# A transformer layer with 32 experts: fetching the first expert's rows before the last block of rows is routed, and reading four sums of an expert together

## The chip, the cores and the metric

The kernel runs on one core of one Trainium2 chip. The metric is device microseconds of one execution, lower is better. Three runs of the kernel before took 2155.97, 2157.39 and 2163.31 us (median 2157.39). One more execution was profiled.

## The reference

One decoder layer on 1024 rows (tokens) of 1024 numbers, all in float32. The part that matters here is the second half: a router picks 4 of 32 experts for each row, and each expert is a gated feed-forward layer over the rows that chose it.

```python
h = rms_norm(x, norm1_g) * (1.0 + scale1) + shift1
proj = h @ w_in                                  # then two kinds of attention
x = x + gate1 * (concat([o_a, o_b]) @ w_out)
h2 = rms_norm(x, norm2_g) * (1.0 + scale2) + shift2
logits = h2 @ w_router + b_router
top_val, top_idx = lax.top_k(logits, 4)          # of 32 experts
gates = softmax(top_val)
# for each expert e, on the rows xe that chose it:
gu = xe @ w_gate_up[e] + b_gate_up[e]            # 1024 -> 2048
g, u = minimum(gu[:, :1024], 7), clip(gu[:, 1024:], -7, 7)
act = (u + 1) * (g * sigmoid(1.702 * g))
y_e = act @ w_down[e] + b_down[e]                # 1024 -> 1024
x = x + gate2 * sum over the chosen experts of gates * y_e
```

## The kernel before

The kernel has four stages: the input projection, attention, a loop over eight blocks of 128 rows, and a loop over the 32 experts. On PE, ACT, DVE and SP (which issues the large loads) instructions run in the order in which the code is written (`tc.manual_schedule`). POOL's order is not written out, a scheduler chooses it from the dependences. Within its engine every instruction runs in order, and whoever waits holds up all that stands behind it.

**The block loop** (L1008 to L1050, class `Block` from L853). Per block b, PE makes the output projection (`products`, L872: 48 matmuls of 512 columns), DVE adds the residual (`add`, L882), the second norm's root is taken by POOL (the power at L111, called from `add`), `logits` (L915) gives the router's scores and the four best, and `places` (L938) works out at which place of each expert's list the row stands. A one-hot matrix `hot` (L948) marks which place of expert 0's list each row takes. `listed` (L958) multiplies it with three columns `tg` (row number minus 1024, gate, one) and adds this up over all eight blocks in the PSUM tile `p0`. `counted` (L970) updates the counts, `scattered` (L980) writes (row, gate) pairs into the table `tab` in HBM by four indirect DMAs from POOL. `rows_out` (L911) stores the block's normalized rows `h2` in `h2d` in HBM. These steps of block b are spread over the two following iterations. The tile `pay` holds what the scatters read. It has three buffers, so its first writer in block b, a POOL `iota` (L944), waits until the scatters of block b-3 have ended.

**Between the loops** (L1051 to L1089, then L1343 to L1352). The last block is routed, expert 0's list is read from `p0` (three small DVE operations for each piece of the list, L965 to L968), the experts are sorted by their counts (`key` to `order`, L1071 to L1089: the first expert to run is always expert 0, with room for 172 rows), and expert 0's rows are gathered from `h2d` by two indirect DMAs from POOL, 128 and 44 rows (`stage_g`, L1139). `stage_t` (L1161) transposes them on PE, ACT and DVE split them into a high and a low half (`xx`, L1177 and L1178), POOL makes a bf16 copy `xb` (L1179).

**The expert loop** (L1355 to L1360, `expert`, L1206). Each expert's weights come as 12 chunks of 1 MB: ten into a ring of six buffers (`eraw`), two (`draw`) into buffers of their own. ACT turns half a chunk at a time into a rounded copy `hb` (L826), DVE takes the remainder `ha` (L813). Buffers are freed by that, and SP's next load waits for it (`pump`, L833, called from `done`). PE then runs five groups of `products` (L1186: 64 matmuls on `hb`, L1196, and 32 times two on `ha`, L1202), and between the fourth and the fifth the "plain half": four of the eight output pieces of the down projection straight from `draw` (L1252), 64 matmuls in two rounds `kh` over pieces j of 0 to 3. The four sums lie in one PSUM tile `pg`, two to a bank. In the second round ACT reads the pieces 0 and 1 into `yl` as soon as they are complete (L1263), and the pieces 2 and 3 after their own matmuls. The tile framework orders reads and writes by tile, so PE's matmuls for j of 2 wait for the reads of j of 0 and 1. PSUM is handed out as four tiles of two banks in turn (`banks`, L1116). `between` calls `stage_t` of the next expert, and `later` puts the last transposes and the scatter of an expert into the next one.

At the end a loop over rows that found no room (L1372) runs as many times as a register loaded at L1371 says, here not at all.

## Time and profile before

| | us |
|---|---|
| median of three runs | 2157.39 |
| profiled execution | 2155.82 |
| span of its instructions | 2154.0 |
| PE busy, of the span | 2046.7 (95%) |
| DVE, ACT, POOL busy | 1631.7, 1357.8, 481.7 |
| share of the 16 DMA engines, 862 to 2100 us | 0.96, at 318 GB/s |

The span runs from the first to the last instruction. The attention ends near 585 us, the block loop runs to 719 us, the first expert's first product starts at 745.96 us, the last scatter is issued at 2142 us. PE is the busiest engine. A busy PE says little about its speed, since matmuls overlap and the granted clock has two levels (1.2 and 2.4 GHz: 0.5 and 1.0 in the views). So the places where PE waits, and the stretches at the lower clock, are what to look for.

### The profile page before, as it was taken

Reading aid. Unit: us, or ns where it says so; the run is one execution under the profiler, and the core shown is the slowest. Engines: PE = TensorE matmul, PEld = TensorE weight load, DVE = VectorE, ACT = ScalarE, POOL = GpSimd, SP = SyncE. Lnnn points to the kernel's source line nnn. Section 1 sums busy time; section 2 is a strip of 40 time slices with the busy share of each in tenths; the row PEclk is TensorE's granted clock in tenths of the full one; section 3 lists DMA queues with packets and bytes.
Section 4 is the critical chain, followed back from the end, with each engine's and each line's share of the span. In section 5 each row is a group of like instructions: output and inputs, shape, how many; then the busy total and the mean of one; then the engine's idle time right before and its main releaser. Section 6 shows DMA issues by size and latency. Waiting matters only on the chain.

```text
span 2154.0 us, 43837 instructions
## 1 busy us (share of the span) xinstructions
PE 2046.7 (95%) x16922; PEld 1914.8 (89%) x16922; DVE 1631.7 (76%) x2838; ACT 1357.8 (63%) x2391; POOL 481.7 (22%) x466
## 2 busy tenths in 40 slices
PE   6999999999999699999999999999999999999997
PEld 6877778998887599999998999999999999999996
DVE  6587765776666778788787877878878878878884
ACT  3522314777643367677677677777877777768774
POOL 2245532111013411112111222112111211211211
PEclk9999999999999799999999999999999999999998
DMA  8267886442233498899799999989999999999993
GB/s 296 67 161 220 217 237 164 112 114 70 90 129 145 158 338 293 268 337 343 268 295 347 289 315 317 324 296 349 309 321 300 355 319 330 325 332 322 332 321 81
DMA packets 273655, 549.53 MB, mean 255 GB/s; under 512 B 31796, under 2 KB 31812, under 8 KB 273316
## 3 DMA queue, kind: packets, MB, share of 16 engines
q1 hardware_dynamic: 251507, 490.61, 67.4%
q0 software_dynamic: 21936, 56.09, 11.2%
q8 instruction: 134, 2.20, 0.4%
q14 instruction: 78, 0.63, 0.1%
HBM read 501.84 MB, written 44.78 MB: 254 GB/s over the span
## 4 chain that ended last, share of the span: by engine, by line
PE 61%; ACT 5%; DMA 3%; DVE 3%; issue 2%; POOL 1%; POOLq 0%; SPq 0%; ACTq 0%; DVEq 0%
PE gu L1196 30%; PE gu L1202 13%; PE gu L1252 10%; PE gu L1285 2%; ACT hb L826 2%; PE gu L1174 2%; PE po L605 1%; ACT yl L1263 1%; DMA eraw<-in_w_down_dram 1%; DMA eraw<-in_w_gate_up_dram 1%; PE pss L567 1%; DMA tab<-pay,sli 1%; PE pt L598 1%; POOL tab L982 1%; DVE ha L813 0%
## 5 line engine op out<-in xcount | busy, mean ns | idle before, releaser
L813 DVE TENSOR_TENSOR ha<-eraw,hb 128x1024 bf16<-128x1024 f32 x640 | 760.0, 1240 | 7.7 <-ACT hb L826 7.7
L826 ACT ACTIVATE hb<-eraw 128x1024 fp32r<-128x1024 f32 x640 | 634.1, 1050 | 21.2 <-DMA eraw<-in_w_down_dram 15.3
L1196 PE MATMUL gu<-xx,hb 128*128 128x256 f32 (+13 forms) x4096 | 586.3, 299 | 2.2 <-DVE xx L1178 2.2
L1196 PEld LDWEIGHTS gu<-xx,hb 128*128 128x128 f32 x4096 | 552.9, 189 | 2.6 <-DVE xx L1178 2.4
L1202 PEld LDWEIGHTS <-ha 128*128 128x128 bf16 x5120 | 310.6, 97 | 11.8 <-issue 1.5
L1252 PE MATMUL gu<-ay,draw 128*128 128x128 f32 (+19 forms) x2048 | 277.9, 292 | 36.4 <-ACT yl L1263 32.9
L1252 PEld LDWEIGHTS gu<-ay,draw 128*128 128x128 f32 x2048 | 260.5, 192 | 44.5 <-ACT yl L1263 39.7
L1202 PE MATMUL gu<-xb,ha 128*128 128x128 bf16 (+19 forms) x4096 | 271.6, 224 | 0.0
L1216 ACT ACTIVATE tb<-gu,bcol 128x128 f32<-128x128 f32 (+19 forms) x512 | 156.9, 369 | 89.8 <-PE gu L1202 80.8
L1182 POOL DMA_INDIRECT out_dram<-y,slot x47 | 79.7, 1695 | 404.9 <-ACT y L1286 263.0
L1146 POOL DMA_INDIRECT xg<-h2d,slot x47 | 65.9, 1401 | 393.0 <-PE gu L1174 86.8
L1196 PE MATMUL gu<-ax,hb 128*128 128x256 f32 (+13 forms) x1024 | 144.5, 298 | 0.0
L1276 ACT ACTIVATE tb<-gu,bcol,g2c 128x128 f32<-128x128 f32 (+19 forms) x128 | 56.3, 465 | 132.4 <-PE gu L1202 104.8
L1196 PEld LDWEIGHTS gu<-ax,hb 128*128 128x128 f32 x1024 | 137.4, 188 | 0.6
L571 DVE CUSTOM_DVE_ANT_0 p<-pss,bias 128x1024 f32<-128x1024 f32 (+7 forms) x128 | 94.4, 755 | 52.1 <-ACT p L580 23.5
L1277 DVE SCALAR_TENSOR_TENSOR ay<-gu,g2c,tb 128x128 f32<-128x128 f32 (+19 forms) x128 | 46.2, 362 | 113.9 <-ACT tb L1276 113.9
L1258 POOL CAST ab<-ax 128x512 bf16<-128x512 f32 (+19 forms) x64 | 69.7, 1094 | 263.7 <-ACT ax L1256 263.7
L605 PE MATMUL po<-vsb,pT 128*128 128x64 f32 (+1 forms) x864 | 111.3, 275 | 2.9 <-ACT pT L599 1.4
L605 PEld LDWEIGHTS po<-vsb,pT 128*128 128x128 f32 x864 | 105.4, 194 | 5.8 <-ACT pT L599 2.0
L580 ACT ACTIVATE p<-p,mn 128x1024 f32<-128x1024 f32 (+7 forms) x128 | 98.6, 773 | 11.9 <-DVE mn L571 11.2
L111 POOL TENSOR_TENSOR rrs<-vrs,nhalf 128x8 f32<-128x8 f32 (+2 forms) x48 | 66.1, 1377 | 169.6 <-DVE vrs L109 167.8
L459 PE MATMUL pp<-wh,hb 128*128 128x512 f32 x240 | 100.5, 419 | 0.0
(275 smaller groups left out, 3080.6 us busy)
## 6 DMA issues: line engine op xcount, KB each, us to landing
eraw<-in_w_gate_up_dram SPq DMA_DIRECT2D x256, 1024.0 KB
draw<-in_w_down_dram SPq DMA_DIRECT2D x64, 1024.0 KB
eraw<-in_w_down_dram SPq DMA_DIRECT2D x64, 1024.0 KB
wraw<-in_w_ada_dram SPq DMA_DIRECT2D x32, 512.0 KB
wraw<-in_w_in_dram SPq DMA_DIRECT2D x23, 512.0 KB
hb<-in_w_ada_dram SPq DMA_DIRECT2D x16, 512.0 KB
qd<-tt POOLq DMA_DIRECT2D x32, 256.0 KB, 3.7
kd<-tt POOLq DMA_DIRECT2D x32, 256.0 KB, 4.0
```

The source lines that it names most:

```text
L459: nc.tensor.matmul(pp, hh[b][:, k], wh[:, kk], start=(k == 0), stop=False)
L571: nc.vector.tensor_tensor_reduce(p[:, :n], pss[:, :n], bias[:, (NB - 1 - ib) * P:(NB - 1 - ib) * P + n], -1.0, 3.0e38, OP.add, OP.min, mn)
L580: nc.scalar.activation(p, p, AF.Exp, bias=self.mn[c], scale=-1.0, accum_out=self.l[:, c:c + 1])
L605: nc.tensor.matmul(self.po[:, :w], self.pT[:, k], vsb[self.br][:, k, self.h * w:(self.h + 1) * w], start=(k == 0), stop=(k == self.ib))
L813: nc.vector.tensor_tensor(parts[t][1], raws[c][:, 2 * q:2 * q + 2], parts[t][0].bitcast(F32), OP.subtract)
L826: nc.scalar.activation(h_, raws[c][:, 2 * q:2 * q + 2], AF.Copy)
L1182: nc.gpsimd.indirect_dma_start(out=out, out_offset=bass.IndirectOffsetOnAxis(ap=sl.bitcast(I32)[:n, 0:1], axis=0), in_=y[:n], in_offset=No ...
L1196: nc.tensor.matmul(pg[j // 2][:, j % 2, :max(256, 2 * C)], w[k][0][:, j * P:(j + 1) * P], xk[k], start=(k == 0), stop=False)
L1202: nc.tensor.matmul(pg[j // 2][:, j % 2, C:2 * C], w[k][1][:, j * P:(j + 1) * P], xb[:, k], start=False, stop=(k == KT - 1))
L1216: nc.scalar.activation(t[:, j], p[:, j, C:2 * C], AF.Identity, bias=bc[:, f + j:f + j + 1], scale=1.0)
L1252: nc.tensor.matmul(place(j), raw[:, k, j * P:(j + 1) * P], a[:, 4 * kh + k], start=(kh + k + j % 2 == 0), stop=(kh == 1 and k == 3 and j % ...
L1258: nc.gpsimd.tensor_copy(ab[:, f], ah[:, f, :C].bitcast(F32))
```

## The change

Three edits.

1. **Expert 0's rows come in two parts.** `listed` now adds up the blocks 0 to 6 only, before the last block is routed. Inside the last `add` the sums are copied to `sums0`, and two lists `early0`, `early1` are made from them (`slots_of`). Two indirect DMAs gather the rows of these lists at once into `xg0`. Places that belong to a row of block 7, or to none, fetch rows 1024 and up of `h2d`, which are zeros. `stage_0` then adds up in PSUM the transposes of the gathered rows (matmuls with the identity) and block 7's own rows times its one-hot matrix (`cur.h2` times `cur.hot`), 32 matmuls in place of 16 transposes. The complete list (`slots0`), the sorting of the experts and the rest follow after that. For it, the last block's `h2` and `hot` and the gathered rows live in `hb` buffers, and `pay` and `sli` have eight buffers, one per block. The rows of `h2d` that belong to block 7 are set to zero once, early.
2. **The plain half's four sums are read together**, after the loop over j.
3. **The register of the overflow loop is loaded before expert 5**, not at the end.

```diff
@@ table, add, places, listed, counted @@
+                nc.sync.dma_start(h2d[S - P:S, :], z)
...
+            def slots_of(sums, tiles):
+
+                for i, (t0, n) in enumerate(BLOCKS0):
+                    sl, c = tiles[i], 3 * i
+                    nc.vector.tensor_scalar(sl[:n, 0:1], sums[:n, c:c + 1], pcol[:n], float(S), op0=OP.add, op1=OP.add)
+                    nc.vector.scalar_tensor_tensor(sl.bitcast(I32)[:n, 0:1], sums[:n, c + 2:c + 3], pneg[:n], sl[:n, 0:1],
+                                                   op0=OP.mult, op1=OP.add)
...
                     nc.scalar.activation(sq, self.x1[:, c], AF.Square, accum_out=self.s2[:, n:n + 1])
+                    if mid:
+                        mid()
...
-                    self.h2 = ro.tile([P, D], F32, name="h2", bufs=1)
+                    self.h2 = ro.tile([P, D], F32, name="h2", bufs=1) if self.b < NB - 1 else slot(False).bitcast(F32)
...
-                    pay = (sm if self.b < NB - 1 else rt).tile([P, TOPK, 2], F32, name="pay")
+                    pay = rt.tile([P, TOPK, 2], F32, name="pay", bufs=NB)
...
-                                         stop=(self.b == NB - 1 and i == len(BLOCKS0) - 1))
-                    if self.b == NB - 1:
...
+                                         stop=(self.b == NB - 2 and i == len(BLOCKS0) - 1))
...
-                    self.sli = (sm if self.b < NB - 1 else rt).tile([P, TOPK], I32, name="sli")
+                    self.sli = rt.tile([P, TOPK], I32, name="sli", bufs=NB)
@@ after the block loop @@
             cur.products(1, range(PZ, 8))
+            pv.listed()
             cur.turn_x1(0)
-            cur.add(1)
-            pv.listed()
+            early = [rt.tile([P, 2], F32, name=f"early{i}") for i in range(len(BLOCKS0))]
+
+            def fetch_list():
+                nc.vector.tensor_copy(sums0, p0[:, :3 * len(BLOCKS0)])
+                slots_of(sums0, early)
+
+            cur.add(1, fetch_list)
+            xg0 = []
+            for (t0, n), sl in zip(BLOCKS0, early):
+                xg0.append(slot(False).bitcast(F32))
+                nc.gpsimd.indirect_dma_start(out=xg0[-1][:n], out_offset=None, in_=h2d,
+                                             in_offset=bass.IndirectOffsetOnAxis(ap=sl.bitcast(I32)[:n, 0:1], axis=0))
...
             cur.places()
-            cur.listed()
             pump(2)
             cur.counted()
             pump(4)
-
-
-            pc = ps3.tile([P, 512], F32, name="po")[:, :E]
...
+        def stage_0(st):
+
+            st["x"] = operand(C0, "xx", "xb")
+            bc = st["bc"]
+            nc.vector.tensor_mul(bc[:, 2 * KT:], bc[:, 2 * KT:], g2c)
+            pts = [banks().rearrange("p g (k c) -> p (g k) c", k=4) for _ in BLOCKS0]
+            for (t0, n), xg, pt in zip(BLOCKS0, xg0, pts):
+                for k in range(KT):
+                    nc.tensor.matmul(pt[:, k, :n], xg[:n, k * P:(k + 1) * P], ident[:n, :n], start=(k % 4 == 0), stop=False)
+            for (t0, n), pt in zip(BLOCKS0, pts):
+                for k in range(KT):
+                    nc.tensor.matmul(pt[:, k, :n], cur.h2[:, k * P:(k + 1) * P], cur.hot[:, t0:t0 + n],
+                                     start=False, stop=(k % 4 == 3))
+                operand_of(st, t0, n, pt)
@@ expert @@
-                    if kh and j % 2:
-                        if j == 1:
-                            yl = ap_.tile([P, 4, C], F32, name="yl")
-                        for f in (j - 1, j):
-                            nc.scalar.activation(yl[:, f], place(f), AF.Identity,
-                                                 bias=bc[:, 2 * KT + f:2 * KT + f + 1], scale=g2c[:, f:f + 1])
-                    if j == 1:
                         done()
+                if kh:
+                    yl = ap_.tile([P, 4, C], F32, name="yl")
+                    for f in range(4):
+                        nc.scalar.activation(yl[:, f], place(f), AF.Identity,
+                                             bias=bc[:, 2 * KT + f:2 * KT + f + 1], scale=g2c[:, f:f + 1])
@@ between the loops @@
-        st = stage_g(0)
+        st = {"C": C0, "bc": cols.pop(0), "blocks": BLOCKS0, "slots": slots.pop(0)}
+        stage_0(st)
         cur.scattered()
-        stage_t(st, 0)
-        stage_t(st, 1)
+        pl = banks()[:, 0]
+        for i, (t0, n) in enumerate(BLOCKS0):
+            nc.tensor.matmul(pl[:, 3 * i:3 * i + 3], cur.hot[:, t0:t0 + P], cur.tg, start=(i == 0), stop=(i == len(BLOCKS0) - 1))
+        nc.vector.tensor_add(sums0, sums0, pl[:, :3 * len(BLOCKS0)])
+        slots_of(sums0, slots0)
...
+        pc = banks()[:, 0, :E]
...
+            if i == 5:
+                n_over = nc.values_load(tot[0:1, 0:1], min_val=0, max_val=P)
```

How this moves instructions is shown at three places. First ACT, in the plain half of the first expert, in the kernel before (`yl`: the four sums, `hb`: half chunks of weights, `xx`: the next expert's operand).

```order
L1256 ACTIVATE ax<-ay 128x4x172
L1263 ACTIVATE yl<-gu,bcol,g2c 128x172 x2
L826 ACTIVATE hb<-eraw 128x1024
L1263 ACTIVATE yl<-gu,bcol,g2c 128x172 x2
L826 ACTIVATE hb<-eraw 128x1024
```

And in the changed kernel, whose line numbers are its own:

```order
L1269 ACTIVATE ax<-ay 128x4x172
L836 ACTIVATE hb<-eraw 128x1024
L1276 ACTIVATE yl<-gu,bcol,g2c 128x172 x4
L836 ACTIVATE hb<-eraw 128x1024
L1175 ACTIVATE xx<-gu 128x8x128
```

All four reads now stand behind one half chunk and in front of the next.

Second POOL, from the last blocks of the block loop to the first expert, before (`rr`: the norm's power, `tab`: the scatters of a block, `xg`: the gathers of expert 0's rows).

```order
L982 DMA tab<-pay,sli 36864x2 x4
L111 TENSOR_TENSOR rr_7253<-vr_7251,nhalf 128x1
L982 DMA tab<-pay,sli 36864x2 x4
L111 TENSOR_TENSOR rr_7418<-vr_7416,nhalf 128x1
L982 DMA tab<-pay,sli 36864x2 x4
L1146 DMA xg<-h2d,slots_2975 128x1024
L1146 DMA xg<-h2d,slots_2976 44x1024
L982 DMA tab<-pay,sli 36864x2 x4
```

The same place in the changed kernel (the gathers write `hb` buffers):

```order
L988 DMA tab<-pay,sli 36864x2 x4
L111 TENSOR_TENSOR rr_7255<-vr_7253,nhalf 128x1
L988 DMA tab<-pay,sli 36864x2 x4
L1072 DMA hb<-h2d,early_7413 128x1024
L111 TENSOR_TENSOR rr_7429<-vr_7427,nhalf 128x1
L1072 DMA hb<-h2d,early_7414 44x1024
L988 DMA tab<-pay,sli 36864x2 x8
```

The gathers stand ahead of the last eight scatters, around the last block's power. The `iota` of `pay`, which stood between a block's scatters and the next power four times, is at the program's start for all blocks.

Third SP at the end of the block loop, with the semaphores that each load or store waits for, before.

```order
L892 DMA out_dram<-osb 128x1024 [waits DMAHW2_49,DVE_49]
L913 DMA h2d<-h_7441 128x1024 [waits DMAHW7_49,DVE_49]
L1107 DMA bcol<-in_b_exp_t_dram 128x24 [waits DMAHW0_49]
L796 DMA eraw_7562<-in_w_gate_up_dram 128x4x512 [waits DMAHW4_49,DMAHW1_49,DMAHW6_49,PE_49,Activation_49]
L796 DMA eraw<-in_w_gate_up_dram 128x4x512 [waits DVE_49]
```

And in the changed kernel:

```order
L904 DMA out_dram<-osb 128x1024 [waits DMAHW3_49,DVE_49]
L925 DMA h2d<-hb 128x1024 [waits DMASW7_49,DMAHW0_49,DMASW6_49,DVE_49]
L1102 DMA bcol<-in_b_exp_t_dram 128x24 [waits DMAHW1_49]
L806 DMA eraw_7546<-in_w_gate_up_dram 128x4x512 [waits DMAHW5_49,DMAHW2_49,DMAHW7_49,PE_49,Activation_49]
L806 DMA eraw<-in_w_gate_up_dram 128x4x512 [waits DVE_49]
```

The order is the same, but the store of block 7's rows has two more waits (DMASW7 and DMASW6, DMAs issued by POOL): both gathers must have ended, since they read the same HBM tensor.

## Rows read from the trace of the kernel before

**Rows 1.** The page's costliest groups: busy us, mean ns, idle before, releaser

```profile
L1252 PE MATMUL gu<-ay,draw 128*128 128x128 f32 (+19 forms) x2048 | 277.9, 292 | 36.4 <-ACT yl L1263 32.9
```

**Rows 2.** Who waited for whom, PE, 760 to 2100: total, times, longest

```profile
PE gu L1252 <- ACT yl L1263: 32.1, 31, 3.2
PE gu L1252 <- DVE ay L1238: 2.5, 2, 2.1
```

**Rows 3.** Timeline of PE, plain half of the fourth expert: start, us, instruction, idle before

```profile
929.13 2.05 PE L1252 MATMUL gu<-ay,draw 128*128 128x128 f32 x16 [0.90 <-ACT yl L1263]
931.01 0.94 PE L1174 MATMUL gu<-ident,xg 128*128 128x128 f32 x8
931.88 4.06 PE L1196 MATMUL gu<-ax,hb 128*128 128x256 f32 x32
```

**Rows 4.** Timeline of ACT and DVE at the same place

```profile
931.22 0.81 ACT L1263 ACTIVATE yl<-gu,bcol,g2c 128x128 f32<-128x128 f32 x2 [1.20 <-PE gu L1252]
932.86 1.13 ACT L1177 ACTIVATE xx<-gu 128x1024 fp32r<-128x1024 f32 x2
...
934.28 1.34 DVE L1178 TENSOR_TENSOR xx<-gu,xx 128x1024 fp32r<-128x1024 f32 x2
```

**Rows 5.** Busy time by stretch: PE, PEld, DVE, ACT, POOL, clock, DMA, GB/s

```profile
921.70:962.30 40.60, 39.70 (x411) 38.86 (x409) 35.48 (x49) 31.97 (x54) 6.01 (x6) 1.00 1.01 355
...
756.00:776.00 20.00, 20.00 (x167) 19.63 (x166) 16.52 (x21) 15.15 (x22) 0.00 (x0) 1.00 1.05 383
```

**Rows 6.** Who waited for whom, ACT, 760 to 2100

```profile
ACT hb L826 <- DMA eraw<-in_w_down_dram: 15.3, 10, 7.6
```

**Rows 7.** Who waited for whom, POOL, 560 to 720

```profile
POOL pay L944 <- DMA tab<-pay,sli: 10.5, 4, 3.2
```

**Rows 8.** Timeline of DVE in one block of the loop

```profile
654.78 0.17 DVE L109 TENSOR_SCALAR vrs<-ss 128x4 f32<-128x4 f32 x1 [1.25 <-ACT sq L694]
657.06 0.16 DVE L115 TENSOR_TENSOR qr<-rr 128x1 f32<-128x1 f32 x1 [2.10 <-POOL rr L111]
```

**Rows 9.** Timeline of PE in the same block

```profile
658.67 0.58 PE L960 MATMUL p<-tg,hot 128*128 128x3 f32 x4 [2.31 <-DVE tg L955]
```

**Rows 10.** Who waited for whom, PE, 540 to 760

```profile
PE p L960 <- DVE tg L955: 6.2, 5, 2.3
```

**Rows 11.** Busy time by stretch, two iterations of the block loop

```profile
656.00:674.00 18.00, 15.69 (x82) 13.08 (x81) 11.06 (x35) 6.17 (x22) 6.23 (x9) 0.91 0.40 147
...
692.00:710.00 18.00, 16.59 (x77) 14.03 (x76) 12.29 (x43) 4.89 (x14) 6.26 (x10) 0.81 0.42 138
```

**Rows 12.** Timeline of DVE and POOL between the two loops

```profile
720.46 0.69 DVE L886 TENSOR_TENSOR osb<-osb,t 128x512 f32<-128x512 f32 x1
730.41 0.22 DVE L966 SCALAR_TENSOR_TENSOR slots<-p,pneg,slots 128x1 int32<-128x1 f32 x1
...
722.44 0.57 POOL L111 TENSOR_TENSOR rr<-vr,nhalf 128x1 f32<-128x1 f32 x1 [2.17 <-DVE vr L109]
732.27 1.02 POOL L1146 DMA_INDIRECT xg<-h2d,slots  x1 [2.11 <-DMA h2d<-h]
733.60 1.66 POOL L1146 DMA_INDIRECT xg<-h2d,slots  x1 [0.31 <-DVE mcum L978]
```

**Rows 13.** Timeline of PE between the two loops

```profile
738.03 1.08 PE L1174 MATMUL gu<-ident,xg 128*128 128x128 f32 x4 [4.04 <-DMA xg<-h2d,slots]
741.49 2.25 PE L1174 MATMUL gu<-ident,xg 44*128 44x44 f32 x12 [2.37 <-DMA xg<-h2d,slots]
745.96 6.86 PE L1196 MATMUL gu<-xx,hb 128*128 128x344 f32 x32 [2.22 <-DVE xx L1178]
```

**Rows 14.** Chain of waits between the two loops: start, us, what

```profile
743.20 1.03 ACT xx L1177
```

**Rows 15.** Timeline of SP's issues at the end of the block loop

```profile
728.09 0.32 SPq L913 DMA_DIRECT2D h2d<-h  x1
729.27 5.57 SPq L796 DMA_DIRECT2D eraw<-in_w_gate_up_dram  x2
```

More of the change, by code (lines that the diff above doesn't have):

```diff
@@ L658, in hybrid_layer @@
             slots0 = [rt.tile([P, 2], F32, name=f"slots0{i}") for i in range(len(BLOCKS0))]
+            sums0 = rt.tile([P, 3 * len(BLOCKS0)], F32, name="sums0")
             dgc = rt.tile([P, 1], F32, name="dgc")
@@ L942, in places @@
                     nc.vector.reciprocal(self.den, self.den)
-                    pay = (sm if self.b < NB - 1 else rt).tile([P, TOPK, 2], F32, name="pay")
+                    pay = rt.tile([P, TOPK, 2], F32, name="pay", bufs=NB)
                     nc.gpsimd.iota(pay.bitcast(I32)[:, :, 0], pattern=[[0, TOPK]], base=self.b * P, channel_multiplier=1)
                     nc.vector.tensor_scalar_mul(pay[:, :, 1], self.ge, self.den)
-                    hot = sm.tile([P, len(BLOCKS0) * P], F32, name="hot", bufs=2)
+                    hot = (sm.tile([P, len(BLOCKS0) * P], F32, name="hot", bufs=2) if self.b < NB - 1
+                           else slot(False).bitcast(F32)[:, :len(BLOCKS0) * P])
                     nc.vector.tensor_scalar(hot, srow, pp[:, 0:1], self.msk[:, 0:1], op0=OP.is_equal, op1=OP.mult)
-                    tg = sm.tile([P, 3], F32, name="tg")
+                    tg = (sm if self.b < NB - 1 else rt).tile([P, 3], F32, name="tg")
                     nc.gpsimd.iota(tg[:, 0:1], pattern=[[0, 1]], base=self.b * P - S, channel_multiplier=1,
@@ L1068, in hybrid_layer @@
             pump(4)
-            pc = ps3.tile([P, 512], F32, name="po")[:, :E]
-            nc.tensor.matmul(pc, ones, mcum, start=True, stop=True)
-            key = rt.tile([P, 2, E], F32, name="key")
-            nc.vector.tensor_scalar(key[:, 0], pc, float(E), float(E - 1), op0=OP.mult, op1=OP.add)
-            nc.vector.tensor_sub(key[:, 0], key[:, 0], erow)
-            nc.vector.tensor_scalar_add(key[:, 0, 0:1], key[:, 0, 0:1], -4096.0 * E)
-            skey = rt.tile([P, E], F32, name="skey")
-            for i in range(E // 8):
-                nc.vector.max(skey[:, 8 * i:8 * i + 8], key[:, i % 2])
-                if i + 1 < E // 8:
-                    nc.vector.match_replace(key[:, (i + 1) % 2], skey[:, 8 * i:8 * i + 8], key[:, i % 2], -1.0e9)
-            ki = rt.tile([P, E], I32, name="ki")
-            nc.vector.tensor_copy(ki, skey)
-            order = rt.tile([P, E], I32, name="order")
-            nc.vector.tensor_single_scalar(order, ki, E - 1, op=OP.bitwise_and)
-            nc.vector.tensor_scalar(order, order, -1.0, float(E - 1), op0=OP.mult, op1=OP.add)
-            orderf = rt.tile([P, E], F32, name="orderf")
-            nc.vector.tensor_copy(orderf, order)
     with ExitStack() as se:
@@ L1345, in hybrid_layer @@
         pump(PB)
-        st = stage_g(0)
+        st = {"C": C0, "bc": cols.pop(0), "blocks": BLOCKS0, "slots": slots.pop(0)}
+        stage_0(st)
         cur.scattered()
-        stage_t(st, 0)
-        stage_t(st, 1)
+        pl = banks()[:, 0]
[3 more added lines that the diff above has]
+        slots_of(sums0, slots0)
+        for i, (t0, n) in enumerate(BLOCKS0):
+            nc.vector.tensor_copy(slots0[i][:n, 1:2], sums0[:n, 3 * i + 1:3 * i + 2])
+        pc = banks()[:, 0, :E]
+        nc.tensor.matmul(pc, ones, mcum, start=True, stop=True)
+        key = rt.tile([P, 2, E], F32, name="key")
+        nc.vector.tensor_scalar(key[:, 0], pc, float(E), float(E - 1), op0=OP.mult, op1=OP.add)
+        nc.vector.tensor_sub(key[:, 0], key[:, 0], erow)
+        nc.vector.tensor_scalar_add(key[:, 0, 0:1], key[:, 0, 0:1], -4096.0 * E)
+        skey = rt.tile([P, E], F32, name="skey")
+        for i in range(E // 8):
+            nc.vector.max(skey[:, 8 * i:8 * i + 8], key[:, i % 2])
+            if i + 1 < E // 8:
+                nc.vector.match_replace(key[:, (i + 1) % 2], skey[:, 8 * i:8 * i + 8], key[:, i % 2], -1.0e9)
+        ki = rt.tile([P, E], I32, name="ki")
+        nc.vector.tensor_copy(ki, skey)
+        order = rt.tile([P, E], I32, name="order")
+        nc.vector.tensor_single_scalar(order, ki, E - 1, op=OP.bitwise_and)
+        nc.vector.tensor_scalar(order, order, -1.0, float(E - 1), op0=OP.mult, op1=OP.add)
+        orderf = rt.tile([P, E], F32, name="orderf")
+        nc.vector.tensor_copy(orderf, order)
         lists(1)
```

21 lines of the change are left out of this document (8 added, 13 removed).

## The prediction

> **What bounds the kernel now.** I read the page first: PE is busy for most of the span, so the question is what ends its idle time. Among the page's costliest groups one row of PE has idle time worth speaking of: the matmuls of the plain half sat idle for 36.4 us, 32.9 us of it until ACT had read `yl` [rows 1]. The waits of PE over the expert loop say the same: 32.1 us in 31 waits on `yl`, and next to nothing else [rows 2]. So the expert loop is bound by PE, with one stall per expert. The timeline shows it: 16 matmuls (j of 2 and 3) start 0.90 us late, behind two reads of 0.81 us [rows 3, 4]. Nothing else waits there, since j of 2 and 3 write another bank of the same tile.
>
> The busy time by stretch shows the next limit. In the expert that starts its plain half at 921.7 us the DMA engines are full (share 1.01) at 355 GB/s; over the 20 us after 756 us they moved 383 GB/s [rows 5]. ACT waited 15.3 us for one kind of chunk [rows 6], and PE's other waits there, 2.5 us on `ay` [rows 2], are what such a late chunk leaves.
>
> Ahead of the experts I read two places. In the block loop PE waits for `tg`, 6.2 us in 5 waits [rows 10], and the granted clock falls behind two of them [rows 11]. Between the loops PE waits for the two gathers, and the first product starts at 745.96 us [rows 13].
>
> **The plain half.** Removed: the stall in each of 32 experts. Of the 32.9 us, the longest wait was 3.2 us and one more was near 2 us, where ACT itself was late; those two keep about 3.3 us beyond the usual 0.9. That leaves 29.6 us. Added: ACT now reads four pieces after j of 3, 4 x 0.41 = 1.6 us, where it read two in 0.81 us [rows 4]. Three things could wait for that.
> - PSUM: where the next expert has two row blocks, the second tile of the following products is the one `yl` is read from. PE reaches it after the transposes (0.87 us from 931.01 to 931.88) and 8 of the 32 products in 4.06 us (1.0 us), so 1.9 us after j of 3; the reads end after 1.65 us [rows 3, 4]. It just passes.
> - The next operand `xx`: ACT's `xx` starts after `yl` and one half chunk, at the same time as before, and DVE ends at 935.62 [rows 4]. PE wants it after its down products, 2 us later than that before, now 1 us. It passes.
> - The half chunk formerly behind the first two reads now stands ahead of all four; it falls into the time in which ACT waited for PE.
> I count 0.5 us for all three over the loop, 0 to 5 us.
>
> Given back to the DMA: the stall was also 0.9 us in which loads ran ahead. A short expert (120 rows or so) moved 40.6 x 355 = 14.4 MB; at 383 GB/s that takes 37.6 us, so the 39.7 us now wanted are possible, with 2 us to spare [rows 5]. But where ACT already waited for chunks (15.3 us in 10 waits), every later chunk is missed by up to 0.9 us more, so I take 4 us. Bounds: 0, and 14 us if all 15 short experts gain nothing (15 x 0.93).
>
> The Trainium skill, "DMA: Bandwidth & Descriptors", section "Where 436 GB/s comes from", says that HBM to SBUF transfers are bound by a limit of about 358 GB/s for each core. This trace differs: 383 GB/s over 20 us [rows 5]. By that limit 14.4 MB take 40.3 us, a short expert gains 0.3 in place of 0.9 us, and the sum would be some 5 us worse than mine. "HBM Reference", specifications, puts a core that streams alone near 425 GB/s, which agrees better with the row.
>
> **The block loop.** Only a side effect of the buffers: `pay` has eight, so its `iota` no longer waits for scatters. That wait held POOL for 10.5 us in four blocks [rows 7], and the power stands behind it. In the block shown DVE waited 2.10 us for the power, until 657.06 [rows 8], and PE 2.31 us for `tg`, which DVE makes from it [rows 9]. Now the power starts when its input is there, before 654. Late next is the root of the other norm: DVE reaches its input at 654.78 + 0.17 [rows 8], so `tg` comes 2.1 us earlier and PE waits 0.2 us. PE's five waits are 6.2 us, of which one of 1.2 us lies behind the loop; 5.0 us lie here [rows 10], less 4 x 0.2 leaves 4.2 us. The clock: 0.81 over 18 us means 6.8 us at 1.2 GHz, 0.91 means 3.2 us [rows 11]. Half of each is lost, 3.4 + 1.6 = 5.0 us, since PE has work all through. The wait at 658.67 [rows 9] lies just ahead of the drop in the first of these stretches, so I take the drops to go with the waits. Together 9.2 us; bounds 0 (another wait takes the place) and 10.
>
> **Between the loops.** Block 7's residual ends at 720.46 + 0.69 = 721.15. Then DVE makes the early lists: a copy and four operations of 0.25 us (the pace at 730.41) end near 722.3. That delays DVE's chain of the last block by 1.2 us at most. POOL starts the first gather near 722.0; the power follows at 723.4 in place of 722.44 [rows 12], behind the gather's 1.02 us, and DVE has the 1.2 us of `h2`'s product to do meanwhile. The second gather starts near 724.2. Before, the gathers started at 732.27 and 733.60 [rows 12] and their rows were there at 738.03 and 741.49 [rows 13], 5.8 and 7.9 us after. So the second lands at 730.0 to 732.1; I take 732.1, the row of the same gather. Block 7's `h2` was stored at 728.09 [rows 15], so even 1.2 us later it is there first and doesn't decide. From there 16 pieces on PE (8 transposes of the small block, 8 products with `hot`) at 0.23 us, between the 0.27 and 0.19 of [rows 13], then ACT's `xx`. From its start at 743.20 [rows 14] to the first product at 745.96 it took 2.76 us. 732.1 + 3.7 + 2.8 = 738.6, so 7.4 us earlier.
>
> What is late next: DVE now sorts the experts after this, 13 operations of 0.25 us or 3.2 us ahead of the remainders `ha` that the first product's second part needs: 0.7 us by my estimate. And the loads don't move up as much as PE. The store of block 7's rows waits for both gathers, to 732 in place of 728.09, and the two chunk loads behind it on SP (729.27) move with it [rows 15]; the next chunks follow DVE's remainders, some 2 to 3 us earlier than before, while PE is 7 us earlier. DMA ran full from 756 us [rows 5], so ACT waits for the chunks of the down projection, and PE for what its lead doesn't cover: an estimate of 1.5 us. Net 5 us; bounds 0 and 9.5.
>
> **The register.** Each engine loads it once, before expert 5, about 0.5 us on PE. At the end it was beside other work. +0.5 us.
>
> **Sum.** 29.6 - 0.5 - 4 + 9.2 + 5 - 0.5 = 38.8 us. Against the profiled execution's own 2155.8 us that is 2117.0; the median of the runs lies 1.6 us above it, so 2118 us.
>
> **The rivals.**
> - DMA takes the bound in the short experts. For: share 1.01 there [rows 5], ACT's waits [rows 6]. Against: 383 GB/s when more was asked. The 15 short experts gain nothing: 14 us are lost in place of 4: 2128 us. The limit of 358 GB/s of the Trainium skill ("DMA: Bandwidth & Descriptors", as above) would be this mechanism at half its price, 2123 us.
> - The front parts give nothing: another wait holds `tg`, or the gathers land late behind the scatters. For: chains of small operations have many ends. Against: the power's releaser is named [rows 7, 8], and the order puts the gathers first. 2118 + 9 = 2127 us without the block loop's part, 2132 without both.
> - More than I take: the DMA gives nothing back and the two late places heal, 4 + 3 + 4 us: 2107 us.
> - Slower than before: late chunks drop the clock. A wait of 2.31 us was followed by 3.2 us at half speed [rows 9, 11]. If each of the 15 short experts made PE wait 3 us for a chunk and then lose 1.6 us, that is 70 us: 2118 + 70 - 4 = 2184 us. It decides from 2.6 us for each short expert (39 / 15). Against: 14.4 MB in 42.7 us is 337 GB/s, 12% below the best stretch [rows 5].
>
> **How the numbers follow.** My forecast has 0.56, with a range of its own from 2111 to 2124; the DMA 0.17, the front parts 0.13, more 0.10, slower 0.04. The range that should hold 8 in 10 runs from 2104 (the case of more, and the second gather at 730.0) to 2137 (neither front part, and 5 us of waits behind `yl`). A change of 0.3%, 6.5 us, is what can be told from none. Every case but the last gains more; I leave 0.03 for several small losses together: faster 0.93, same 0.03, slower 0.04.
>
> **What would show it.** Right: no idle time of the plain half's matmuls on `yl`; the DMA share in the expert loop a little higher with more waits of ACT for chunks; POOL's power directly behind a block's scatters, waits for `tg` under 0.5 us and a clock of 1.0 through the block loop; the first product near 739 us. Wrong: PE waiting on `yl` in the products that follow, or for `ay` or `gt` behind late chunks in many short experts; a first product after 743 us; the store of block 7's rows issued after 735 us.

## The result, and the profile after

The changed kernel took 2104.76 us (median of 4 runs, 2103.2 to 2107.2), the kernel before 2158.26 us (4 runs): ratio 0.975, interval 0.973 to 0.977. The forecast was 2118 us, so the sign was right and the gain was 13 us larger than I had it, at the low end of my range (2104 to 2137 us). The profiled execution took 2107.2 us, its span 2105.4; against 2155.82 us that is 48.6 us less. It divides by the starts and ends of rows of PE's timelines (us):

| stretch | before | after | difference |
|---|---|---|---|
| start to the block loop's first product (L878, now L888) | 586.13 | 588.73 | +2.6 |
| first to last product of the block loop | 133.6 | 127.5 | -6.1 |
| from there to expert 0's first product | 26.3 | 19.0 | -7.3 |
| from there to the first plain half | 31.7 | 30.6 | -1.0 |
| the 32 plain halves (L1252, now L1265), each from its first to its last matmul | 328.5 | 287.6 | -40.9 |
| what lies between two plain halves, 31 times | | | +3.6 |
| the rest | | | +0.5 |

The first line is the stretch up to the end of the attention. The changed kernel's profile has one more fall of the granted clock there (362.9 to 366.3 us), and PE's waits around it are the same. Over the 14 traces below this stretch took 583.5 to 586.1 us without edit 1 and 583.6 to 590.0 us with it. Whether the change has a part in that is not shown.

The plain half's row of the page's costliest groups, to hold against [rows 1]:

```profile
L1265 PE MATMUL gu<-ay,draw 128*128 128x128 f32 (+19 forms) x2048 | 268.2, 289 | 4.1 <-DVE ay L1251 4.1
```

PE's waits over the same stretch as in [rows 2] (total, times, longest):

```profile
PE gu L1265 <- DVE ay L1251: 4.1, 4, 2.2
PE gu L1209 <- DVE xx L1176: 1.8, 3, 0.8
PE gu L1209 <- DVE ax L1270: 0.7, 1, 0.7
...
PE gu L1215 <- POOL ab L1271: 0.2, 1, 0.2
```

The wait on `yl` is gone. In its place stand 1.6 us more on `ay`, and 2.7 us on `xx`, `ax` and `ab`, operands that ACT and DVE finish late. PE and ACT at the plain half of the fourth expert, as in [rows 3, 4]:

```profile
906.29 3.79 PE L1265 MATMUL gu<-ay,draw 128*128 128x128 f32 x32
909.91 0.94 PE L1168 MATMUL gu<-ident,xg 128*128 128x128 f32 x8
910.78 3.84 PE L1265 MATMUL gu<-ay,draw 128*128 128x128 f32 x32
914.46 0.94 PE L1168 MATMUL gu<-ident,xg 128*128 128x128 f32 x8
```

```profile
914.66 1.51 ACT L1276 ACTIVATE yl<-gu,bcol,g2c 128x128 f32<-128x128 f32 x4 [1.15 <-PE gu L1265]
```

The second round is now one unbroken run, and the four reads lie beside PE's transposes. The x32 counts records of the profile. Each of these fp32 matmuls stands as two: 32 matmuls for each of 32 experts in the code, x2048 in the page's row. So the 64 matmuls of the plain half, as I counted them ahead, are 32 matmuls with 64 records, and the 16 behind the stall in [rows 3] are eight.

ACT's waits for chunks (against [rows 6]), and the busy time by stretch near the two places of [rows 5], with the columns as there:

```profile
ACT hb L836 <- DMA eraw<-in_w_down_dram: 27.8, 17, 5.5
ACT hb L836 <- DMA eraw<-in_w_gate_up_dram: 5.8, 5, 2.4
```

```profile
743.00:763.00 20.00, 20.00 (x165) 19.76 (x163) 18.95 (x24) 12.06 (x20) 3.38 (x2) 1.00 0.98 359
745.30:765.30 20.00, 20.00 (x174) 19.64 (x173) 18.11 (x24) 12.07 (x20) 2.15 (x2) 1.00 1.05 386
910.00:949.50 39.50, 39.50 (x409) 38.86 (x408) 35.52 (x50) 31.72 (x53) 7.98 (x7) 1.00 1.01 356
```

A short expert is 1.1 us faster (39.5 us for 40.6), yet the DMA moved no more in a second than before (356 GB/s for 355): the loads fall behind, and ACT's waits for the down projection's chunks nearly doubled. Over 20 us at the start of the expert loop it still moves 386 GB/s, as before (383); the window that begins 2.3 us earlier, with a share of 0.98, shows 359.

The block loop: POOL's power stands right behind the scatters (against [rows 7, 8]), and PE's waits from 585 to 746 us (against [rows 10]):

```profile
652.74 1.40 POOL L988 DMA_INDIRECT tab<-pay,sli  x1 [0.30 <-issue]
654.60 0.57 POOL L111 TENSOR_TENSOR rr<-vr,nhalf 128x1 f32<-128x1 f32 x1 [0.46 <-DVE s L905]
```

```profile
PE po L952 <- DVE nm L945: 3.6, 2, 1.8
...
PE p L973 <- DVE tg L968: 0.2, 1, 0.2
```

The waits on `tg` are all but gone (0.2 us); the router's scores (`nm`) hold `places` twice, once in the last iteration and once behind the loop. The clock still falls, as in [rows 11]:

```profile
655.00:673.00 18.00, 17.83 (x93) 14.80 (x91) 11.66 (x40) 8.04 (x28) 6.89 (x10) 0.91 0.43 158
710.00:728.00 18.00, 14.38 (x63) 12.67 (x63) 13.81 (x54) 6.72 (x14) 11.72 (x10) 0.62 0.34 116
```

Between the loops, POOL, SP and PE (against [rows 12, 13, 15]):

```profile
719.08 1.01 POOL L1072 DMA_INDIRECT hb<-h2d,early  x1 [3.02 <-PE pt L913]
720.09 0.59 POOL L111 TENSOR_TENSOR rr<-vr,nhalf 128x1 f32<-128x1 f32 x1
720.90 1.65 POOL L1072 DMA_INDIRECT hb<-h2d,early  x1 [0.22 <-issue]
```

```profile
725.70 0.32 SPq L925 DMA_DIRECT2D h2d<-hb  x1
```

```profile
724.05 0.64 PE L952 MATMUL po<-msk,upper 128*128 128x32 f32 x2 [1.84 <-DVE nm L945]
...
724.93 5.46 PE L1187 MATMUL gu<-ident,hb 128*128 128x128 f32 x32
730.32 3.77 PE L1190 MATMUL gu<-hb 128*128 128x128 f32 x32
735.24 5.33 PE L1209 MATMUL gu<-xx,hb 128*128 128x344 f32 x32 [0.49 <-DVE xx L1176]
```

The store of block 7's rows waits for both gathers and is issued at 725.70, so the second gather, started at 720.90, took at most 4.8 us. PE doesn't wait for it. The 32 matmuls that make expert 0's rows stand as 64 records, two each, and take 9.2 us.

### The profile page after: what moved, and what is told of

Its sections match the earlier page's. It is cut to its first block, busy times and chain, and to the rows that moved or that the text cites. A ratio compares the mean times of both kernels' runs of the same rounds, so it can differ in the third digit from the quotient of the medians.

```text
span 2105.4 us, 43924 instructions
## 1 busy us (share of the span) xinstructions
PE 2043.5 (97%) x16970; PEld 1917.5 (91%) x16970; DVE 1636.7 (78%) x2844; ACT 1356.1 (64%) x2391; POOL 499.1 (24%) x466
## 4 chain that ended last, share of the span: by engine, by line
PE 60%; DVE 6%; DMA 4%; ACT 3%; issue 2%; POOL 0%; ACTq 0%; POOLq 0%; SPq 0%; DVEq 0%
PE gu L1209 29%; PE gu L1215 13%; PE gu L1265 11%; DMA eraw<-in_w_down_dram 2%; PE gu L1296 2%; PE gu L1168 2%; DVE ha L823 1%; PE po L605 1%; DMA eraw<-in_w_gate_up_dram 1%; PE pss L567 1%; ACT hb L836 1%; PE pt L598 1%; ACT sq L696 0%; DVE osb L896 0%; DVE t L895 0%
## 5 line engine op out<-in xcount | busy, mean ns | idle before, releaser
L1265 PE MATMUL gu<-ay,draw 128*128 128x128 f32 (+19 forms) x2048 | 268.2, 289 | 4.1 <-DVE ay L1251 4.1
L1265 PEld LDWEIGHTS gu<-ay,draw 128*128 128x128 f32 x2048 | 257.4, 191 | 5.7 <-DVE ay L1251 5.2
L1141 POOL DMA_INDIRECT xg<-h2d,slot x47 | 71.5, 1521 | 340.1 <-DMA slot<-tab 79.3
L571 DVE CUSTOM_DVE_ANT_0 p<-pss,bias 128x1024 f32<-128x1024 f32 (+7 forms) x128 | 94.6, 755 | 53.8 <-ACT p L580 22.2
L580 ACT ACTIVATE p<-p,mn 128x1024 f32<-128x1024 f32 (+7 forms) x128 | 98.7, 774 | 12.2 <-DVE mn L571 11.5
```

What stands on the lines that cost most here:

```text
L571: nc.vector.tensor_tensor_reduce(p[:, :n], pss[:, :n], bias[:, (NB - 1 - ib) * P:(NB - 1 - ib) * P + n], -1.0, 3.0e38, OP.add, OP.min, mn)
L580: nc.scalar.activation(p, p, AF.Exp, bias=self.mn[c], scale=-1.0, accum_out=self.l[:, c:c + 1])
L1141: nc.gpsimd.indirect_dma_start(out=xg[:n], out_offset=None, in_=h2d, in_offset=bass.IndirectOffsetOnAxis(ap=sl.bitcast(I32)[:n, 0:1], axis=0))
L1265: nc.tensor.matmul(place(j), raw[:, k, j * P:(j + 1) * P], a[:, 4 * kh + k], start=(kh + k + j % 2 == 0), stop=(kh == 1 and k == 3 and j % ...
```

## The experiments

Each ratio is to runs of the kernel before on the same chip, with its 95% interval in brackets; their medians were 2153.66 us beside the first four, 2155.59 beside the next four and 2152.78 beside the last four.

**The plain half.**

e1, the kernel before with edit 2 alone:

```diff
-                    if kh and j % 2:
-                        if j == 1:
-                            yl = ap_.tile([P, 4, C], F32, name="yl")
-                        for f in (j - 1, j):
+                if kh:
+                    yl = ap_.tile([P, 4, C], F32, name="yl")
+                    for f in range(4):
                         nc.scalar.activation(yl[:, f], place(f), AF.Identity,
```

> The kernel before with edit 2 alone: the plain half's four sums are read together. Theory A (a stall costs the time from start to start): where PE waits for `yl`, it loses the idle time of the row and the refill of its pipeline too, about 1.15 us in each of 32 experts, 37 us; the rest of the loop gives back 0 to 4 us. Expected 2158 - 35 = 2123 us (2118 to 2128), and each plain half 1.05 to 1.3 us shorter from first to last matmul. Theory B (only the idle time is lost, 0.93 us): 30 us less 4 given back, 2132 us, and each plain half 0.9 us shorter; then 10 us of what the changed kernel gained would be the front parts'.

Measured: 2118.76 us, ratio 0.9844 (0.9824 to 0.9863), that is 33.6 us less (29.5 to 37.9). The plain halves are 39.9 us shorter, most of them by 1.08 to 1.28 us; the rest of the loop is 5.8 us longer. That is theory A; theory B's 0.9 us for each plain half, and its 26 us in all, are out.

e2, the changed kernel with the old reads (the diff the other way round):

> The changed kernel with the old reads (two sums behind j of 1, two behind j of 3). Theory A: the stall comes back whole, 2105 + 35 = 2140 us (2135 to 2145), and the edits 1 and 3 alone are worth 13 to 18 us against the kernel before. Theory B: 2105 + 26 = 2131 us. In both PE's waits on `yl` are near 32 us in the trace, the first product stays near 735 us.

Measured: 2138.92 us, ratio 0.9937 (0.9919 to 0.9954): the edits 1 and 3 with the buffers are worth 13.6 us (9.9 to 17.4). PE waited 31.0 us on `yl`. The plain halves are 37.0 us longer than in the changed kernel. The two parts make 33.6 + 13.6 = 47.2 us. The whole change came to 54 us (50 to 58) in the first comparison and to 48 us (44 to 51) when it was repeated (e9), so the parts add up to the second, and the 6 us between the two comparisons are open.

e3, the four sums in two tiles:

```diff
-            pg = banks()
-                return pg[:, j // 2, j % 2 * 256:j % 2 * 256 + C]
+            pg = [banks() for _ in range(2)]
+                return pg[j // 2][:, 0, j % 2 * 256:j % 2 * 256 + C]
```

> The kernel before, where the plain half's four sums lie in two PSUM tiles of two banks (one bank of each is used), read two at a time as before. Theory (the stall is the tile's: PE's matmuls for j of 2 wait only since the reads are of the same tile): the waits on `yl` are gone as with edit 2, 2118 to 2128 us. Rival 1 (ACT's reads hold PE for themselves, or the stall is one of accumulating groups): the waits stay, 2158 us. Rival 2 (the tile taken in addition is missed): no wait on `yl`, but waits of PE on a `gu` tile ahead of the next transposes or products, 0.5 us or more in each expert with two row blocks, 2130 to 2145 us.

Measured: 2124.62 us, ratio 0.9862 (0.9844 to 0.9881). No wait on `yl` is left, with the reads where they were: the stall was the tile's. The plain halves are 38.2 us shorter, but the rest of the loop is 8.2 us longer. PE's waits from 760 to 2100 us tell why:

```profile
PE gu L1196 <- DVE xx L1178: 4.2, 12, 0.6
PE gu L1174 <- DVE su L1218: 4.0, 3, 1.5
```

So rival 2 is true as well, at a small price: the transposes (L1174) now get a tile whose reader on DVE is late, though only three times.

e4, the two early reads made twice:

```diff
-                        for f in (j - 1, j):
+                        for f in (j - 1, j, j - 1, j) if j == 1 else (j - 1, j):
```

> The kernel before, where the two reads behind j of 1 are made twice (the same values): the stall is lengthened from about 0.93 to 1.74 us of idle time, by 0.81 us. Theory A (a fixed refill beside the idle time): 32 x 0.81 = 26 us more, 2184 us, and the plain half 0.81 us longer. If the loss were proportional to the idle time, 1.15 / 0.93 x 26 = 32 us, 2190 us. If the loads bound the 15 short experts, they would hide their share: 14 us, 2172 us.

Measured: 2175.87 us, ratio 1.0107 (1.009 to 1.0125), 23 us more. The fourth expert's plain half on PE, which was [rows 3] before:

```profile
925.90 2.05 PE L1252 MATMUL gu<-ay,draw 128*128 128x128 f32 x16
929.55 2.05 PE L1252 MATMUL gu<-ay,draw 128*128 128x128 f32 x16 [1.60 <-ACT yl L1263]
```

This is the cleanest test. (The idle time grew by 0.70 us, where I expected 0.81.) The plain half of the fourth expert lasts 8.34 us without a stall (after), 9.50 with 0.90 us of idle time (before), 10.20 with 1.60 (e4). What it loses beyond the idle time is 0.26 us both times: 9.50 - 8.34 - 0.90 and 10.20 - 8.34 - 1.60. In 28 of the 32 experts it is 0.24 to 0.27 us. A stall costs its idle time and a fixed restart, as theory A has it; it is not proportional. The rest of the loop changed by 0.5 us, so the loads hid little of it; three plain halves that had waited longer before (the 9th, 13th and 21st) are 3.3 us shorter together.

**The loads.** e8, where two of each expert's twelve chunks are loaded by half and a part of the weights is left out:

```diff
+HALF = (2, 8)                        # of an expert's 12 chunks, from the third expert on
-                nc.sync.dma_start(raws[d], ...)
+                nc.sync.dma_start(raws[d][:, :2 if few(d) else 4], ...)
```

> The changed kernel with two of each expert's twelve chunks loaded by half only (from the third expert on; the half that is there is used twice, so a part of the weights is left out): 11 MB for each expert in place of 12. Theory C (PE bounds the experts, and late chunks cost only what the plain half's gain gave back): ACT's waits for chunks fall from 36 us to under 8, PE's waits on `ay` (4.1 us) and on `xx` go, and the time falls by 4 to 8 us, to 2097 to 2101 us by the earlier runs. Theory D (the loads bound the 15 short experts of the changed kernel): each of these could shorten by up to a twelfth of its 39.5 us, 3.3 us, so 15 to 50 us less.

Measured: 2102.69 us, ratio 0.9758 (0.9734 to 0.9781), not to be told from the changed kernel by the time; its attention and the stretch ahead of the experts happened to be 2.4 us longer. In the trace the plain halves are 4.4 us shorter and the rest of the expert loop 2.1 us: 6.5 us. PE's and ACT's waits, 760 to 2100 us:

```profile
PE gu L1271 <- DVE ay L1257: 0.4, 1, 0.4
```

```profile
ACT hb L842 <- DMA eraw<-in_w_down_dram: 18.6, 12, 4.5
...
ACT hb L842 <- DMA eraw<-in_w_gate_up_dram: 1.6, 1, 1.6
```

Theory C: the waits on `ay` go (4.1 to 0.4 us), and a twelfth less to load is worth 6.5 us in the trace, not 15 to 50. ACT's own waits for chunks fell less than I expected (33.6 to 20.2 us, where I said under 8). Most of them reach no one: PE's waits in this stretch are 2.9 us in all.

**The block loop.** e5, the kernel before with eight buffers, and e6, the changed kernel with the old ones:

```diff
-                    pay = (sm if self.b < NB - 1 else rt).tile([P, TOPK, 2], F32, name="pay")
+                    pay = rt.tile([P, TOPK, 2], F32, name="pay", bufs=NB)      # e5; sli the same; e6 the reverse
```

> The kernel before with eight buffers for `pay` and `sli` and nothing else. Theory: POOL's `iota` no longer waits for scatters, the waits of PE on `tg` in the block loop go, and the loop from its first to its last product takes 127 us in place of 133.4 (what the changed kernel shows): 6 us less in all, ratio to before 0.997. Rival 1 (the side effect that I took, with the stretches at the lower clock gone as well): 9 us less. Rival 2 (another wait of the block loop takes the whole place, and the 6 us of the changed kernel come from its other edits): no change, the loop stays at 133 us.

> The changed kernel with `pay` and `sli` in their old buffers (three, and one of its own for the last block). Theory: the waits on `tg` come back, 4 to 5 us in the block loop, which takes 133 us again; 6 us more than the changed kernel, ratio to before 0.980 or 0.981. Rival: the loop stays near 127 us, since early lists or another edit freed it.

Measured: e5 2145.38 us, ratio 0.9957 (0.9944 to 0.997), 9.3 us less (6.5 to 12.1); e6 2111.67 us, ratio 0.9802 (0.9777 to 0.9828). The loop took 126.2 us in e5 and 134.2 in e6. Over all traces it splits by the buffers alone: 132.9 to 134.2 us in five with the old ones, 126.2 to 127.5 in six with eight (124.9 to 126.4 in the three with eight and PZ 7, below). So this side effect is 6.7 us of the gain by the loop's length, and it needs no other edit. By the time alone e5 lies at rival 1's 9 us, and its interval ends at the theory's ratio of 0.997; its trace, with a loop 7.4 us shorter than in the kernel before, lies between the two. Taken from e2's 13.6 us, e5's 9.3 leave about 4 us for the edits 1 and 3.

What the clock does in this loop is another matter. The kernels e5 and e9 (the changed kernel once more, below) show no fall in it at all:

```profile
655.00:673.00 18.00, 17.69 (x97) 13.98 (x95) 12.44 (x41) 6.84 (x23) 6.91 (x9) 1.00 0.41 147
```

That row is of e9, the same program as above with its 0.91. So the falls are not set by the program alone. Over the 14 traces, a fit of the loop's length gives 122.1 us + 1.34 for each us of PE's idle time + 0.33 for each us at half clock (0.5 in the views), and all lie within about 0.4 us of it: half clock costs a third of its length there, not the half that I took.

e7, one number changed. PZ says how many pieces of the last output projection's second half PE runs ahead of block 6's places, so two more now stand ahead of them:

```diff
-PZ = 5
+PZ = 7
```

> The changed kernel, where in the last iteration of the block loop the places of block 6 stand behind three more pieces of the product... of the seven pieces before them in place of five, so behind two more (PZ 7 for 5). Theory (the wait of 1.8 us on `nm` is short of work that PE could do first): it falls to about 0.4 us, the products end 1 us earlier, and so do the early lists and the gathers: 1 us less in all. Rival 1 (the sums then wait for `hot` and `tg`, since only one piece is left behind the places): the wait moves there, no change. Rival 2 (the stretch at the lower clock near 714 to 728 us goes with this wait): it is gone too, 3 to 6 us less.

Measured: 2101.19 us, ratio 0.9756 (0.9734 to 0.9778). The wait is 0.39 us in place of 1.78, the loop 124.9 us in place of 126.2 to 127.5. The clock fell at 715 us nonetheless (until 722 us): rival 2 is out. By the time alone e7 can't be told from the changed kernel.

**Between the loops.** e9, the changed kernel again:

> The changed kernel once more, beside the three that follow: ratio to before 0.975 to 0.978, block loop near 127 us, 19 to 20 us from its last product to the first product of expert 0, plain halves without a wait on `yl`. Where the clock falls it may differ from the first profile: the falls stood at other times in each kernel so far.

Measured: 2106.46 us, ratio 0.9779 (0.9764 to 0.9794). From the last product of the loop to expert 0's first product it took 24.1 us, not 19.0. PE's timeline there:

```profile
721.86 0.64 PE L952 MATMUL po<-msk,upper 128*128 128x32 f32 x2 [3.84 <-DVE nm L945]
...
722.74 7.33 PE L1187 MATMUL gu<-ident,hb 128*128 128x128 f32 x32
730.00 7.05 PE L1190 MATMUL gu<-hb 128*128 128x128 f32 x32
```

The same 64 records took 14.4 us at the granted clock of 0.5, where the first profile had it back at 1.0 from 728 us on and took 9.2. Five traces with the old gathers took 25.6 to 26.3 us for this stretch, six with the early ones 18.6 to 24.1 us. So edit 1 gives 2 to 7 us here, and in this pair of traces of one program the difference goes with where the clock comes back. The repeat's whole gain is also smaller: 47.6 us, against 53.5 in the first comparison's medians.

e10, three small edits on the changed kernel:

```diff
-PZ = 5
+PZ = 7
-            cur.rows_start()
             cur.norm2()
             cur.logits()
+            cur.rows_start()
-                for k in range(KT):       # for each of two pieces of the list
-                    nc.tensor.matmul(pt[:, k, :n], cur.h2[...], cur.hot[:, t0:t0 + n], ...)
+                for k in range(4 * g, 4 * g + 4):     # for each half of the row
+                    nc.tensor.matmul(pt[:, k % 4, :C0], cur.h2[...], cur.hot[:, :C0], ...)
```

> The changed kernel with three small edits that the traces point to: (1) PZ 7 for 5 as in the run before; (2) the first product that makes `h2` of the last block stands behind its router's chain on DVE instead of ahead of it (1.2 us); (3) block 7's one-hot products take the 172 columns at once in 8 matmuls in place of 16 of 128 and 44, into two tiles by halves of the row, so that ACT and DVE start on the first half while PE makes the second. Theory: 2.6 + 0.85 + 1 us, first product 4 us earlier than in the changed kernel, 2100 us by the first runs, ratio to before 0.001 to 0.002 below that of the changed kernel in this call. Rival: the hot matrix comes later by the 1.3 us that `h2` now takes ahead of it and PE waits for it: 1 to 2 us less of the gain.

Measured: 2106.3 us, ratio 0.9783 (0.9769 to 0.9798): no gain. PE's timeline:

```profile
720.63 2.05 PE L1187 MATMUL gu<-ident,hb 128*128 128x128 f32 x8
724.45 5.64 PE L1187 MATMUL gu<-ident,hb 128*128 128x128 f32 x24 [1.76 <-DVE pos L978]
730.02 4.34 PE L1192 MATMUL gu<-hb 128*128 128x172 f32 x16
```

PE stopped after the first tile: by its releaser the second waits for DVE's `pos`, the read of block 7's places (`pp`), so it seems to lie where those stood, and `pos` now stands behind both products of `h2`, 2.5 us. Neither theory nor rival had this wait. The products with the one-hot matrix did get shorter (at half clock 16 records in 4.3 us, where e9 had 32 in 7.05), but the wait took it.

e11, the same with PE kept busy:

```diff
+            fill = ps3.tile([P, 512], F32, name="pm")
+            for k in range(6):
+                nc.tensor.matmul(fill, cur.oh[:, k], cur.oh[:, 0:4].rearrange("p k c -> p (k c)"), ...)
```

> The last kernel, and six matmuls of 512 columns more (1.4 us at the full clock, 2.6 us at half), whose result nobody reads, behind the last router's scores, where PE waits for `nm`. Theory W (the granted clock falls behind PE's waits there, as I took it for the block loop): with the wait filled the clock stays at or comes back to 1.0 ahead of the 48 pieces that make expert 0's rows, which take 7 us in place of 8 to 9; first product 1 to 2 us earlier. Rival: the fall begins ahead of the wait, at small matmuls, and stays: no change, or 0.5 us later.

Measured: 2104.7 us, ratio 0.9776 (0.9762 to 0.9791). The wait on `nm` is filled (`places` starts without idle time), the wait on `pos` is 2.78 us, and the clock fell again at 721.5 us until 731.7. From product to product 22.2 us against 22.0 in e10: the rival, no change. It doesn't settle what lets the clock fall.

e12, expert 0's rows from transposes of the gathered rows alone:

```diff
-                    nc.tensor.matmul(pt[:, k, :n], xg[...], ident[:n, :n], start=(k % 4 == 0), stop=False)
-            ...                                       # the products with cur.hot
+                    nc.tensor.transpose(pt[:, k, :n], xg[...], ident[:n, :n])
```

> The changed kernel with expert 0's rows made from the early gathers alone: 16 transposes in place of 16 matmuls with the identity and 16 with the one-hot matrix (block 7's rows are left out of expert 0). Theory (PE's pieces bound the first product, since the gathers are there before 724.9 us): the 32 pieces took 64 records and 9.2 us, 16 transposes take 16 records and 3 to 4 us; first product 5 to 6 us earlier than in the changed kernel. Rival (the second gather lands after that): PE waits for it, and the first product is 0 to 3 us earlier.

Measured: 2103.6 us, ratio 0.9776 (0.9761 to 0.9792), not to be told from e9 by the time. PE's timeline:

```profile
719.58 1.95 PE L1187 MATMUL gu<-ident,hb 128*128 128x128 f32 x8
722.13 1.08 PE L1187 MATMUL gu<-ident,hb 44*128 44x44 f32 x8 [0.61 <-DVE pos L978]
...
726.99 6.94 PE L1205 MATMUL gu<-xx,hb 128*128 128x344 f32 x32 [2.36 <-DVE xx L1176]
```

These are 16 records and 3.0 us at half clock, in place of 64 records; the stretch from product to product is 16.1 us, 8.0 less than e9, which ran it at half clock too, and 2.9 less than the first profile. PE waited for `xx` and for `pos`, not for a gather. So in the changed kernel PE's pieces bound this place, and the early gathers are there in time.

## Why the prediction was right or wrong, point by point

**The plain half: right mechanism, mis-sized term.** I took 29.6 us from the column of idle time. The plain halves shrank by 40.9 us. PE's idle time in them fell by 31.4 us, from 35.6 to 4.1 (all releasers). The restart adds 0.26 us in each, 8.3 us in 32. In the fourth expert's trace, records follow each other every 0.112 us, and each is modelled as 0.275 us long. The idle column counts from that modelled end, while the loss runs from start to start; and the record behind the first one after the wait starts 0.213 us after it. 0.275 + 0.213 - 2 x 0.112 = 0.26 us. e4 shows that this part is fixed. The other 1.3 us are one fall of the clock at 1326 us in before, absent after, which I can't put down to the change. The Trainium skill, "TensorE: Matmul & The Clock Gate", section "Single matmul latency", gives for a single bf16 matmul a constant of 166 ns at the full clock on top of its columns. That is a cost of the same kind; the fp32 rows here give 0.26 us for a whole stall.

**Behind `yl`: +0.5 taken, 2.7 us seen**, as waits on `xx`, `ax` and `ab`; my 1 us of slack for `xx` was 0.06 to 0.9 us in 18 of the 31 experts that follow another. Before it was not 2 us there but 1.4 to 2.4, and the stall that went was worth 1.2 us, not 0.9.

**Given back to the DMA: about right in size.** I took 4 us. The stretches between plain halves grew by 3.6 us, the 2.7 us above among them, and the waits on `ay` by 1.6. e8 puts what late loads cost in the changed kernel near 6.5 us; 2.5 us of waits on `ay` were there before the change. But the ground I gave was too good: the short expert ran at 356 GB/s, not at 383. The Trainium skill, "DMA: Bandwidth & Descriptors", section "Where 436 GB/s comes from", has HBM to SBUF transfers bound at about 358 GB/s. The short expert's rate is near it in both kernels (355 and 356); the 20 us at the start of the loop are above it (383 and 386). The loss that I derived from it, 0.6 us in each of 15 short experts or 9 us, did not come.

**The block loop: half of it right.** 9.2 us taken, 6.1 measured, 6.7 over eleven traces. The 4.2 us of waits came as 3.1 (5.9 to 2.8 us of PE's idle time from first to last product; the new wait on `nm` keeps 1.8), and with the fitted 1.34 that is 4.2 us of time. The step of my working that failed is "I take the drops to go with the waits": the falls stand at other times in each execution, with and without waits ahead (e7, e9), and cost a third of their length, not half. 5.0 us should have been 1.7 by the fit (5 us less at half clock in the pair of profiles). What lets the clock fall there stays open, and the clock of 1.0 through the loop, one of my signs, did not come (0.91 over 655 to 673 us).

**Between the loops: 7.4 us gross came as 7.3, by other parts.** The second gather took at most 4.8 us, not 7.9, so the rows were there before PE could use them. Against that, 16 pieces of 0.23 us (3.7 us) were in truth 32 matmuls of two records each: 9.2 us, or 14.4 at half clock, for transposes of one record. I priced a matmul with the identity by the row of a transpose. That 7.3 comes so near to 7.4 is luck: the two errors cancelled in that profile; in e9 they did not, and 2 us remained. The 1.5 us of DMA lag and the store after 735 us did not appear (725.70). `ha` held PE for 0.3 us where I took 0.7. The 1.0 us that the stretch behind it gained goes with the clock: the first 32 products of expert 0 took 6.86 us before, at half clock until 749.4 us, and 5.33 us after; in e9, at half clock again until 742.0, they took 7.01 and the gain is gone.

**The register:** 0.5 us taken, nothing seen: the stretches around expert 5 differ by 0.05 us or less.

**The sum:** for the profiled execution I had 2117.0 us, and it took 2107.2, 9.8 us less. The expert loop gave 12.2 us more than I took (37.3 for 25.1); the rest nearly evens out: the two front parts 0.9 us less (13.3 for 14.2), expert 0's first groups 1.0 more, the register 0.5 more, the end 0.5 less, and 2.6 lost in the attention. The other 3 us of the 13 lie between the profiled executions and the medians, which I took to differ by 1.6 us as before; after, the median is 2.4 us below the profiled execution.

The measured time lies next to my rival "more than I take" (2107 us), but not by its mechanism: it had the loads giving nothing back and the late places healed, and the loads did take back what I said. What it stands for is the restart of each stall, which no rival of mine had. The DMA as the bound of the short experts is out (the one shown is 1.1 us faster, and e8 gave 6.5 us, not 15 to 50), and so are front parts that give nothing (13.3 us) and late chunks that make it slower.

## What to carry to other kernels

A stall of PE in a stream of matmuls cost more here than its idle column shows: compare the length from start to start with an unstalled stretch, or lengthen the stall to see the fixed part, before you multiply by the count. Price an operation by its own row, counting records for each instruction; the row of one that looks alike (a transpose for a matmul with the identity) can be off by two or more. Where a tile shared by two halves of a loop causes the stall, later reads and more tiles both remove it, and which is better is decided by who next waits for the tile.

## What the runs showed that I had not expected

- One program's two profiled executions differ by 5 us in one stretch of 20 us: the clock was at 0.5 from 714.5 to 728.1 us in one and from 718.1 to 742.0 in the other. A gain in such a stretch can't be read from one trace.
- DMA shares near 1.0 went with very different rates in the changed kernel: 386 GB/s over the 20 us from 745.3 us (shown above), 356 GB/s over one short expert, 332 GB/s over the 80 us from 1110 us. So a window that begins 2 us off can show another rate, and a limit read from one stretch need not hold in the next.

```profile
1110.00:1190.00 80.00, 77.79 (x761) 75.79 (x759) 67.19 (x86) 63.03 (x100) 18.25 (x15) 1.00 1.01 332
```

- A wait can move by PSUM alone: in e10 and e11 a tile handed out anew held PE for 1.8 and 2.8 us behind a small DVE read of an older tile at the same place.
